# A row sum on one core: the first 128 rows as two loads of half rows

## The chip, the cores and the metric

The kernel runs on one core of a Trainium2 chip. The metric is the device time of one execution in microseconds, the median of several runs. Beside it there is one profiled execution with a trace of every instruction and every DMA packet.

## The reference

The input `x` has 32 x 512 rows of 1024 float32 numbers, 64 MiB in all. Each row is summed and the sum is multiplied by 0.5; the output has 32 x 512 numbers.

```python
def reference(x: np.ndarray, multiplier: float) -> np.ndarray:
    return (np.sum(x, axis=-1) * multiplier).astype(np.float32)
```

## The kernel before, in words

The 16384 rows are taken as 128 partitions x 128 rows. They are worked on in three parts.

**The head** is the first 128 rows, one row for each partition (L112). One load brings it into the tile `head`. ScalarE sums each partition's row with an activation that scales and accumulates (`act_row`, L90) into the first column of the tile `column`, which VectorE has cleared (L113). So that 128 sums can leave in long runs rather than one number for each partition, VectorE transposes `column` in blocks of 32 x 32 into `row` (L117). Of `row`, partitions 0, 32, 64 and 96 then hold 32 sums each, and one store of 4 x 32 numbers brings them out (L188).

**The blocks.** Seven blocks follow: the first of 15 rows for each partition, the others of 16 (64 KiB for each partition). They go through three buffers `xb`. VectorE sums a whole block in one reduction (L136) and scales the sums into `res` (L142); of the seventh block VectorE takes the first eight rows and ScalarE the other eight. The load of a block waits until VectorE has freed the buffer three blocks earlier (`freed`).

**The end.** The eighth block comes in five pieces, smaller and smaller: three into the buffer (`landed_p0` to `landed_p2`) and two into the tile `end` (`landed_e0`, `landed_e1`). Its rows are shared between ScalarE (`act_row`) and VectorE (`dve_sum`, L99, a fused add and reduction). The very last row is cut into three parts that VectorE sums one after the other; the last instruction of the chain is `final`.

All loads and stores are issued by SP, in program order on one queue, with no planner in between. `start_loads_at_entry` (L223) moves those leading loads that wait for nothing (the head and the first three blocks) to the start of the program. After the last load SP issues the early store of the blocks' sums (L184, which waits for VectorE and ScalarE), the head's store (L188), and then the last store (L214), for which it waits until the last sums are there. It ends by waiting for all three stores.

Of the kernel before, what the change touches and what calls it, by code (L numbers as in the profile page):

```python
# [9 lines left out]
def kernel(  # L10
# [13 lines left out]
    nc = tc.nc  # L24
# [4 lines left out]
    P = nc.NUM_PARTITIONS  # L29
    fp32 = mybir.dt.float32  # L30
    ADD = mybir.AluOpType.add

    x_flat = x.flatten_outer_dims()
    N, D = x_flat.shape
    rows = N // P
    out_flat = out.rearrange("b s -> (b s)")
# [5 lines left out]
    Q = 32  # L42
# [1 line left out]
    own = 1 + sum(sizes)  # L44
    x_rows = x_flat[P : P * own, :].rearrange("(p c) d -> p c d", p=P)
    x_last = x_flat[P * own : N, :].rearrange("(p c) d -> p c d", p=P)
    out_head = out_flat[0:P].rearrange("(q c) -> q c", c=Q)
    out_rows = out_flat[P : P * own].rearrange("(p c) -> p c", p=P)
    out_last = out_flat[P * own : N].rearrange("(p c) -> p c", p=P)

    def sbuf(name, *shape):
        return ctx.enter_context(nc.sbuf_tensor(name, list(shape), fp32)).ap()
# [2 lines left out]
    buf = [sbuf(f"xb{i}", P, B, D) for i in range(bufs)]  # L55
    sums = sbuf("sums", P, rows)
    res = sbuf("res", P, rows)
    head = sbuf("head", P, 1, D)
    column = sbuf("column", P, Q)
    row = sbuf("row", P, Q)  # L60
    cuts = [384, 736, D]
    at = 368
    end = sbuf("end", P, at + D - cuts[1])

    def sem(name):
        return nc.alloc_semaphore(name=name)

    dve_done = sem("dve_done")
# [3 lines left out]
    def marks(i, engine):  # L72

        s = dve_done if engine == "dve" else act_done
        i.then_inc(s, 1)
        counts[engine] += 1
        return counts[engine]

    def load(name, dst, src, free=None, behind=None):

        landed = sem(name)
        i = nc.sync.dma_start(out=dst, in_=src)  # L82
        if free is not None:
            i.wait_op(dve_done, free, "sem-ge")
        if behind is not None:
            i.wait_op(behind, 16, "sem-ge")
        i.then_inc(landed, 16)
        return landed

    def act_row(t, r, dst):  # L90
        return nc.scalar.activation(  # L91
            out=t[:, r, :],
            in_=t[:, r, :],
            func=mybir.ActivationFunctionType.Copy,
            scale=mul,
            accum_out=dst,
        )
# [11 lines left out]
            accum_out=dst,  # L109
        )  # L110

    landed_head = load("landed_head", head[:, 0, :], x_flat[0:P, :])  # L112
    cleared = marks(nc.vector.memset(column, 0.0), "dve")  # L113
    nc.scalar.wait_ge(landed_head, 16)
    nc.scalar.wait_ge(dve_done, cleared)
    summed = marks(act_row(head, 0, column[:, 0:1]), "act")
    turned = nc.vector.transpose(out=row, in_=column)  # L117
    turned.wait_op(act_done, summed, "sem-ge")
    marks(turned, "dve")

    freed = []
    blocks = []
    for b, n in enumerate(sizes):
# [9 lines left out]
        h = n if b < n_blocks - 2 else n // 2  # L133
# [3 lines left out]
                out=sums[:, c0 : c0 + h], in_=t[:, 0:h, :], axis=mybir.AxisListType.X  # L137
# [5 lines left out]
            out=res[:, c0 : c0 + h],  # L143
            in_=sums[:, c0 : c0 + h],
            scalar=mul,
            op=mybir.AluOpType.mult,
# [33 lines left out]
            )  # L180
        )
    ]
    nc.sync.wait_ge(dve_done, early_dve)
    early = nc.sync.dma_start(out=out_rows, in_=res[:, 1:own])  # L184
    early.wait_op(act_done, early_act, "sem-ge")
    early_stored = sem("early_stored")
    early.then_inc(early_stored, 16)
    first = nc.sync.dma_start(out=out_head, in_=row[0:P:Q, :])  # L188
    first_stored = sem("first_stored")
    first.then_inc(first_stored, 16)  # L190

    summed_up = sem("summed_up")
    on_act = {1, 4, 7, 9, 13, 14}
# [22 lines left out]
    stored = sem("stored")  # L216
    store.then_inc(stored, 16)
    nc.sync.wait_ge(early_stored, 16)
    nc.sync.wait_ge(first_stored, 16)
    nc.sync.drain()  # L220
    nc.sync.wait_ge(stored, 16)

# [62 lines left out]
```

## Time and profile before

| What | Value |
|---|---|
| median of 3 runs | 160.5 us (160.48 to 160.57) |
| profiled execution, its own time | 160.47 us |
| its span in the trace | 159.2 us |
| moved by DMA | 67.18 MB, mean 422 GB/s over the span |
| time to landing of the head's load | 3.3 us from issue |
| time to landing of the first block's load | 21.2 us from issue |

The span is the part of the execution that the trace covers, from the first instruction to the last; the remaining 1.27 us lie around it. In the profile, DVE is VectorE, ACT is ScalarE, and SPq is the queue of SyncE that issues DMAs. Landing is counted from the issue of a DMA to the moment at which its semaphore is complete. A DMA of 128 partitions is spread over 16 DMA engines, and here each partition's contiguous run is one packet in the trace; every load adds one completion packet of 4 bytes on each of its engines. A share of busy time over 100% in a short stretch comes from counting packets with the stretch in which they start.

### The profile page before, as it was taken

The page shows a single profiled execution, that of the slowest core. Times are in us where ns is not written, and L with a number is a line of the kernel's source. Part 1 is how long each engine was busy: PE and PEld are TensorE (multiplying, and loading weights), DVE is VectorE, ACT ScalarE, POOL GpSimd, SP SyncE. Part 2 cuts the span into 40 slices and gives each one's busy share as a digit, 9 for nine tenths or more (in the row PEclk, how much of TensorE's full clock was granted, in tenths as well). Part 3 has the DMA queues.
Part 4 walks back from the last instruction along what each step waited for, and adds up shares of the span by engine and source line. Part 5 has one row for each costly group of instructions (what it writes and reads, how often), then busy time and mean ns, then how long its engine had stood idle before and what let it go on. Part 6 is the DMA issues. An engine that isn't in the chain of part 4 may idle for free.

```text
span 159.2 us, 131 instructions
## 1 busy us (share of the span) xinstructions
DVE 119.1 (75%) x40; ACT 17.4 (11%) x31; POOL 0.2 (0%) x4
## 2 busy tenths in 40 slices
DVE  0000059995799968999599995999959999598376
ACT  2300000000000000000000000000000000397384
POOL 0000000000000000000000000000000000000000
DMA  9997996996997999969969969969989799798994
GB/s 379 494 401 340 494 527 264 527 527 264 527 461 329 527 395 395 527 280 511 527 264 527 527 264 527 494 296 527 445 346 527 346 445 527 329 453 371 420 401 151
DMA packets 2168, 67.18 MB, mean 422 GB/s; under 512 B 504, under 2 KB 760, under 8 KB 1016
## 3 DMA queue, kind: packets, MB, share of 16 engines
q1 hardware_dynamic: 2168, 67.18, 98.0%
HBM read 67.11 MB, written 0.07 MB: 422 GB/s over the span
## 4 chain that ended last, share of the span: by engine, by line
DMA 74%; DVE 24%; another core or an unknown queue 1%; SPq 1%; issue 0%
DMA xb<-in_x_dram 74%; DVE sums L136 22%; DVE xb L101 1%; SPq L82 1%; DVE end L101 0%; DVE res L142 0%; DVE res L101 0%
## 5 line engine op out<-in xcount | busy, mean ns | idle before, releaser
L136 DVE TENSOR_REDUCE sums<-xb 128x16 f32<-128x16384 f32 (+2 forms) x7 | 110.9, 15849 | 28.4 <-DMA xb<-in_x_dram 28.4
L91 ACT ACTIVATE xb<-xb 128x1024 f32<-128x1024 f32 x14 | 14.6, 1045 | 137.1 <-DMA xb<-in_x_dram 137.1
L101 DVE CUSTOM_DVE_ANT_0 xb<-xb 128x512 f32<-128x512 f32 (+1 forms) x10 | 5.9, 652 | 4.4 <-DMA xb<-in_x_dram 4.4
L91 ACT ACTIVATION_READ_ACCUMULATOR xb<-xb 128x1 f32 x14 | 2.6, 187 | 0.0
L113 DVE MEMSET column<- 128x32 f32 x1 | 0.1, 85 | 3.0 <-PEq L26 3.0
L117 DVE STREAM_TRANSPOSE row<-column 128x32 f32<-128x32 f32 x1 | 0.2, 212 | 2.6 <-ACT head L91 2.6
L91 ACT ACT_TABLE_LOAD x1 | 1.3, 1283 | 3.1 <-DVE column L113 3.1
L142 DVE TENSOR_SCALAR res<-sums 128x16 f32<-128x16 f32 (+2 forms) x7 | 1.2, 174 | 0.2
L91 ACT ACTIVATE head<-head 128x1024 f32<-128x1024 f32 x1 | 1.1, 1056 | 0.0
L101 DVE DVE_READ_ACCUMULATOR2_ANT res<- 128x1 f32 x10 | 0.8, 80 | 0.0
L101 DVE CUSTOM_DVE_ANT_0 end<-end 128x176 f32<-128x176 f32 (+1 forms) x2 | 0.7, 326 | 0.0
L91 ACT ACTIVATION_READ_ACCUMULATOR head<-head 128x1 f32 x1 | 0.2, 186 | 0.0
L101 DVE DVE_READ_ACCUMULATOR2_ANT end<- 128x1 f32 x2 | 0.2, 82 | 0.0
L266 POOL MEMSET const-bfloat16-1.0<- 128x1 bf16 x1 | 0.1, 101 | 0.0
L266 POOL MEMSET const-uint8-127<- 128x1 uint8 x1 | 0.1, 101 | 0.0
L266 POOL MEMSET const-float32-0.0<- 128x1 f32 x1 | 0.1, 98 | 0.2 <-issue 0.2
L266 POOL MEMSET const-float32-1.0<- 128x1 f32 x1 | 0.1, 98 | 0.0
## 6 DMA issues: line engine op xcount, KB each, us to landing
xb<-in_x_dram SPq DMA_DIRECT2D x1, 7680.0 KB, 21.2
xb<-in_x_dram SPq DMA_DIRECT2D x1, 5120.0 KB, 33.6
xb<-in_x_dram SPq DMA_DIRECT2D x1, 2048.0 KB, 36.4
xb<-in_x_dram SPq DMA_DIRECT2D x1, 704.0 KB, 20.8
head<-in_x_dram SPq DMA_DIRECT2D x1, 512.0 KB, 3.3
end<-in_x_dram SPq DMA_DIRECT2D x1, 176.0 KB, 19.2
end<-in_x_dram SPq DMA_DIRECT2D x1, 144.0 KB, 10.8
xb<-in_x_dram SPq DMA_DIRECT2D x6, 40.8
```

The lines of the kernel that those rows point to most:

```text
L82: i = nc.sync.dma_start(out=dst, in_=src)
L91: return nc.scalar.activation(out=t[:, r, :], in_=t[:, r, :], func=mybir.ActivationFunctionType.Copy, scale=mul, accum_out=dst,)
L101: return nc.vector.tensor_tensor_reduce(out=row[:, 0:mid], in0=row[:, 0:mid], in1=row[:, mid:], scale=scale, scalar=0.0, op0=ADD, op1=ADD, ...
L113: cleared = marks(nc.vector.memset(column, 0.0), "dve")
L117: turned = nc.vector.transpose(out=row, in_=column)
L136: nc.vector.reduce_sum(out=sums[:, c0 : c0 + h], in_=t[:, 0:h, :], axis=mybir.AxisListType.X),
L142: scaled = nc.vector.tensor_single_scalar(out=res[:, c0 : c0 + h], in_=sums[:, c0 : c0 + h], scalar=mul, op=mybir.AluOpType.mult,)
L266: nc = _bacc.Bacc("TRN2", target_bir_lowering=False, num_devices=1)
```

## The change

The head comes in by two loads of 64 rows. In each, a partition receives half a row (512 numbers, 2 KB), so that partition `p` of load `h` holds half `p % 2` of row `64 h + p // 2`. ScalarE sums the halves with two activations, one for each load, into the first two columns of `column`. VectorE transposes as before; the sums of the two halves of a row now stand beside each other in one partition of `row`, and one more VectorE addition joins neighbours into `joined`. Two stores of 4 x 16 numbers bring the sums out. They are issued ahead of the early store and its wait, where the one store came behind it. ScalarE waits for VectorE's clearing before it waits for the loads. Both head loads wait for nothing, so they stand at the start of the program, ahead of the three block loads.

```diff
-    out_head = out_flat[0:P].rearrange("(q c) -> q c", c=Q)
+    H = 2
+    half = D // H
+    out_head = out_flat[0:P].rearrange("(h q c) -> h q c", h=H, c=Q // H)
...
-    head = sbuf("head", P, 1, D)
+    head = sbuf("head", P, H, half)
     column = sbuf("column", P, Q)
     row = sbuf("row", P, Q)
+    joined = sbuf("joined", P, Q // H)
...
-    landed_head = load("landed_head", head[:, 0, :], x_flat[0:P, :])
+    landed_head = [
+        load(
+            f"landed_h{h}",
+            head[:, h, :],
+            x_flat[h * P // H : (h + 1) * P // H, :].rearrange("r (s d) -> (r s) d", s=H),
+        )
+        for h in range(H)
+    ]
     cleared = marks(nc.vector.memset(column, 0.0), "dve")
-    nc.scalar.wait_ge(landed_head, 16)
     nc.scalar.wait_ge(dve_done, cleared)
-    summed = marks(act_row(head, 0, column[:, 0:1]), "act")
+    for h in range(H):
+        nc.scalar.wait_ge(landed_head[h], 16)
+        summed = act_row(head, h, column[:, h : h + 1])
+    summed = marks(summed, "act")
     turned = nc.vector.transpose(out=row, in_=column)
     turned.wait_op(act_done, summed, "sem-ge")
-    marks(turned, "dve")
+    turned = marks(turned, "dve")
+    pairs = row.rearrange("p (c s) -> p c s", s=H)
+    both = nc.vector.tensor_tensor(
+        out=joined.rearrange("p (c o) -> p c o", o=1),
+        in0=pairs[:, :, 0:1],
+        in1=pairs[:, :, 1:2],
+        op=ADD,
+    )
+    both.wait_op(dve_done, turned, "sem-ge")
+    marks(both, "dve")
...
+    first_stored = sem("first_stored")
+    for h in range(H):
+        first = nc.sync.dma_start(out=out_head[h], in_=joined[h:P:Q, :])
+        first.then_inc(first_stored, 16)
     nc.sync.wait_ge(dve_done, early_dve)
     early = nc.sync.dma_start(out=out_rows, in_=res[:, 1:own])
     early.wait_op(act_done, early_act, "sem-ge")
     early_stored = sem("early_stored")
     early.then_inc(early_stored, 16)
-    first = nc.sync.dma_start(out=out_head, in_=row[0:P:Q, :])
-    first_stored = sem("first_stored")
-    first.then_inc(first_stored, 16)
...
-    nc.sync.wait_ge(first_stored, 16)
+    nc.sync.wait_ge(first_stored, 16 * H)
```

## The prediction

> **What bounds the kernel now.** I read first the page's busy and queue lines.
>
> ```profile
> span 159.2 us, 131 instructions
> DVE 119.1 (75%) x40; ACT 17.4 (11%) x31; POOL 0.2 (0%) x4
> ...
> q1 hardware_dynamic: 2168, 67.18, 98.0%
> ```
>
> The 16 DMA engines work 98.0% of the span: 156.0 of 159.2 us. No other engine is near that. The missing 3.2 us must be at the two ends, since the answer for DMA from 0 to 1.1 us counts no packet at all, and the time after 157.1 us holds little but the last store. So the time is: start of the stream, plus its length, plus a tail. The start, from the timeline (start, length, engine, line, operation):
>
> ```profile
> 0.00 0.39 SPq L82 DMA_DIRECT2D head<-in_x_dram  x1
> 0.44 1.38 SPq L82 DMA_DIRECT2D xb<-in_x_dram  x3
> 3.12 1.28 ACT L91 ACT_TABLE_LOAD   x1 [3.12 <-DVE column L113]
> 4.41 1.06 ACT L91 ACTIVATE head<-head 128x1024 f32<-128x1024 f32 x1
> 5.59 0.21 DVE L117 STREAM_TRANSPOSE row<-column 128x32 f32<-128x32 f32 x1 [2.56 <-ACT head L91]
> ```
>
> SP issues a load every 0.46 us (1.38 / 3); the first packet starts 1.11 us after the first issue. All compute on `head` is over by 5.8 us. Then the waits:
>
> ```profile
> ACT xb L91 <- DMA xb<-in_x_dram: 137.1, 4, 132.2
> DVE sums L136 <- DMA xb<-in_x_dram: 28.4, 7, 15.8
> ```
>
> VectorE next waits up to 15.8 us for the first block, and ScalarE 132.2 us for its first block row. Last, the end in the timeline:
>
> ```profile
> 147.33 0.64 SPq L188 DMA_DIRECT2D out_dram<-row  x1
> 154.77 0.69 DVE L101 CUSTOM_DVE_ANT_0 xb<-xb 128x512 f32<-128x512 f32 x1 [1.13 <-DMA xb<-in_x_dram]
> 157.36 0.31 DVE L101 CUSTOM_DVE_ANT_0 end<-end 128x145 f32<-128x145 f32 x1
> 157.70 0.34 SPq L214 DMA_DIRECT2D out_dram<-res  x1
> ```
>
> VectorE goes without a pause from the landing of the second last-block piece (154.77) to 157.67, and the very last load lands at 157.27 (issued 146.47, 10.8 us to landing), 0.09 us before the instruction that needs it. Both ends of the tail hang on the stream: a delay of the whole stream passes to the end one for one.
>
> **Prices of the stream.** Two stretches of the DMA view give the cost of a small packet, one the cost of a start. From 22 to 38 us (64 KB packets only), 155.9 to 156.5 us (pieces of 1 to 1.5 KB), and 1.1 to 2.0 us (4 KB packets of `head`), in that order:
>
> ```profile
> DMA packets 106, 6.95 MB, mean 434 GB/s; under 512 B 0, under 2 KB 0, under 8 KB 0
> ```
> ```profile
> DMA packets 204, 0.22 MB, mean 371 GB/s; under 512 B 32, under 2 KB 204, under 8 KB 204
> ## 3 DMA queue, kind: packets, MB, share of 16 engines
> q1 hardware_dynamic: 204, 0.22, 103.5%
> ```
> ```profile
> DMA packets 67, 0.27 MB, mean 305 GB/s; under 512 B 0, under 2 KB 0, under 8 KB 67
> ```
>
> Full rate is 434 GB/s, 27.1 bytes per ns and engine. In the second stretch 16 x 0.6 us x 1.035 = 9.94 us of engine time moved 371 x 0.6 = 222.6 KB, worth 8.21 us at full rate; 1.73 us is left over 204 packets: **8.5 ns a packet** besides its bytes. In the third, 0.9 us at 305 in place of 434 GB/s lost 0.9 x (1 - 305/434) = **0.27 us**: the price of the start.
>
> **The change, part by part.**
>
> *More packets.* The 128 packets of 4 KB become 256 of 2 KB, the bytes stay: 128 x 8.5 / 16 = 0.068 us for each engine, and one more completion packet for each engine, another 0.009. Together +0.08 us. [...]
>
> *A second small load in the start.* Does the stream run dry between the two? The second is issued at 0.44 us, so by the first's 1.11 us its packets can start at 1.55. The first holds 8 packets for each engine, 8 x (2048 / 27.1 + 8.5) = 0.67 us, so it lasts to 1.78 us, or 2.05 with the start's loss: cover of 0.23 to 0.50 us. The block loads move back by one issue, 0.46 us; the first can start at about 0.90 + 1.11 = 2.01, and the halves last to 2.45 us or more: cover of 0.44. If either cover is gone, the stream stands still for the shortfall. But the start's loss itself may grow. No row shows a load of small rows following another at the start. Lower bound: the first packets are half as long, so a part of the loss that goes with packet length may halve, -0.13 us. Upper bound: the second load repeats the loss, +0.27. I take half of it, +0.13, since the loss belongs to the first half microsecond (in the windows view 254 GB/s from 1.1 to 1.6 us, 369 from 1.6 to 2.1), where packets will now be twice as many.
>
> *ScalarE and VectorE.* ScalarE does two activations of 512 in place of one of 1024 (1.06 us and 0.19 for reading the sum): between 1.4 and 2.5 us in all. VectorE gets one addition of 128x16, by the nearest row (L142, 128x16, 0.17 us) about 0.2, behind a wait for its own transpose. Behind these waits on VectorE stands the first block's sum, whose data comes at about 21 us; behind the second activation stands ScalarE's row at 139.85. All of it, with the later start of ScalarE by one issue, is over near 8 us: 13 us of cover, so nothing. Without cover it would be about 1 us.
>
> *The stores of the first rows.* They go before the early store and ahead of its wait, two in place of one: 2 x 0.64 us of SP from 146.80, and the early store is issued near 148.1 instead of 146.91. What comes behind them on SP is the last store, for which SP now waits 9.7 us. All loads are issued before them, and the early store's packets wait behind those until 156.4, so 8 us of cover; without it, up to 1.2 us. Four more packets of 64 bytes and four completions lie behind the last load in the queues and done before the last store at 158.5. Nothing.
>
> *Sum:* 0.08 + 0.13 = +0.21 us on the profiled execution's 160.47 us (span 159.2 and 1.27 around it, which the change has no reason to move): 160.68. The median of the runs is 160.50, 0.03 over the profiled one: **160.7 us**. About 0.2% (0.32 us) is what a measurement of this kernel can tell from no change, so this counts as the same.
>
> **The rivals.**
>
> *The start is paced by packets, not by bytes (slower).* If in the first half microsecond or so an engine gets packets at a fixed pace, as when a 4 KB packet's turn of about 0.16 us (4096 / 27.1 + 8.5) is also the turn of a 2 KB one, each such turn loses 0.08 us. For: the 254 GB/s of the first half microsecond. Against: in the tail 1 to 1.5 KB packets pass at their own 8.5 ns plus bytes, and the last store's 128 packets of 64 bytes all pass between 158.5 and 158.8 us; but the tail's were queued 10 us ahead. It decides from about 3 lost turns (0.24 + 0.08 = 0.32). Six of the first eight give 0.48 + 0.08 = +0.56: 161.1 us; all 16, +1.3: 161.8. A whole second start loss, 0.27 + 0.08 = +0.35, gives 160.9 and belongs here too. Chance 0.38.
>
> *Every load pays its fixed part (slower).* `head` takes 3.3 us to land, 1.2 of it bytes at full rate: 2.1 us fixed. Bare on the stream, a second load would cost +2.1 + 0.08: 162.7. Against it: 13 loads at that price would leave the engines idle for 27 us, and they idle 3.2. Chance 0.02. [...]
>
> *The start gets smoother (faster).* Shorter packets could take away all the start's loss and even out the engines: -0.27 + 0.08 = -0.19, and the last engine goes over from `head` to the first block at 2.93 us where the mean is 2.73 (packet records of the trace); if the small packets close that, -0.2 more: 160.1 us. For: the end waits for the slowest engine. Against: it needs both, and more packets to the same bytes. Chance 0.14.
>
> **The numbers.** The forecast, +0.21 with bounds -0.05 (0.08 - 0.13) to +0.32, has 0.46, and its own range is 160.4 to 160.8 us. Rivals: 0.40 slower, 0.14 faster. The range goes down to 160.3 (half of the faster case's way) and up to 161.3, beyond the six-turn case, and leaves out the far ends of the three rivals, about 2 in 10.
>
> **What would show it.** Right: 128 packets more of 2 KB, the DMA share still 98% with a first half microsecond no slower than 254 GB/s, the first block landing about 0.2 us later, the last store issued near 157.9 us, and VectorE unbroken before it. A gap between the two halves, or a first block that lands over 0.35 us later, shows the slower rival; one that lands earlier, the faster one. I am wrong altogether if the first block lands as forecast and the end has moved otherwise: then the tail or the moved stores hold a cost that I put at nothing.

## The result, and the profile after

The changed kernel takes 162.82 us (median of 6 runs, 162.06 to 163.84), the kernel before 160.53 us beside it (160.48 to 160.57): 1.0152 times as long, 95% interval 1.0128 to 1.0175, or +2.29 us. It has also become unsteady: its runs lie 1.8 us apart, those of the kernel before 0.1. The profiled execution is one of the longer ones, 163.57 us, 3.10 above the profiled 160.47 of before; the profile's differences are to be held against that. In the ratios of this document a run more than 1.5% above the fastest of its kernel counts as slow and is left out; that is one run each of e4 and e9.

The page's busy and queue lines after:

```profile
span 162.2 us, 136 instructions
DVE 119.3 (74%) x41; ACT 17.6 (11%) x33; POOL 0.2 (0%) x4
...
q1 hardware_dynamic: 2320, 67.18, 96.6%
```

The compute engines work as long as before (VectorE 119.3 us and ScalarE 17.6, before it was 119.1 and 17.4). The DMA engines are busy for 96.6% of a longer span: 156.7 us in place of 156.0, but the idle part has grown from 3.2 to 5.5 us. The timeline says where in the program that can be:

```profile
0.00 0.86 SPq L85 DMA_DIRECT2D head<-in_x_dram  x2
0.91 1.38 SPq L85 DMA_DIRECT2D xb<-in_x_dram  x3
3.41 1.28 ACT L94 ACT_TABLE_LOAD   x1 [3.41 <-PEq L26]
4.70 0.63 ACT L94 ACTIVATE head<-head 128x512 f32<-128x512 f32 x1
6.31 0.18 DVE L133 TENSOR_TENSOR joined<-row 128x16 f32<-128x16 f32 x1
...
149.92 1.19 SPq L206 DMA_DIRECT2D out_dram<-joined  x2
157.87 0.69 DVE L104 CUSTOM_DVE_ANT_0 xb<-xb 128x512 f32<-128x512 f32 x1 [1.14 <-DMA xb<-in_x_dram]
160.45 0.31 DVE L104 CUSTOM_DVE_ANT_0 end<-end 128x145 f32<-128x145 f32 x1
160.80 0.34 SPq L236 DMA_DIRECT2D out_dram<-res  x1
```

The head's compute is over by 6.5 us, as forecast. From the start of the last VectorE chain (157.87) to the start of its last piece (160.45) it is 2.58 us, before it was 2.59 (154.77 to 157.36): the tail is the same, 3.1 us later. So all of the loss lies ahead of it. The waits and the time to landing of the first block (7680 KB) put it right at the start:

```profile
DVE sums L157 <- DMA xb<-in_x_dram: 30.8, 7, 18.2
```
```profile
xb<-in_x_dram SPq DMA_DIRECT2D x1, 7680.0 KB, 23.8
```

The same line of the kernel before:

```profile
xb<-in_x_dram SPq DMA_DIRECT2D x1, 7680.0 KB, 21.2
```

The first block lands 23.8 us after its issue at 0.91, at 24.7; before, it was 21.2 after 0.44, at 21.6. These 3.1 us are the whole difference. It is not a matter of all 16 engines. The trace's packet records show when each engine starts the block. The records do not name the engine; a packet of 61440 bytes that starts where another one ends (as at 2.89 + 2.31 = 5.20 us) is taken for the same engine's second, and the sixteen that follow no other such packet are the engines' first ones. Before, these start between 2.59 and 2.93 us; after, fifteen start between 2.64 and 3.30 and **the sixteenth at 6.16 us**. The count of packets in flight says the same: about ten from 2.8 to 3.1 us, fifteen from 3.3 to 6.1, sixteen from then on, where before it was about sixteen all this time. So one engine stands still for about 3 us. The first packets also take longer, 2.71 us in the mean and up to 3.34, where before it was 2.34 and at most 2.46. The block's last packets end between 20.83 and 21.27 us before, and between 21.41 and 24.38 after: the last engine is 3.11 us late, the mean one 1.00. No engine takes over another's rows (each moves eight of the block's 128 packets), so the lag stays: the program's last load ends at 156.88 before and 159.93 after, 3.04 us apart.

### The profile page after: what moved, and what is told of

It is laid out like the page before. It is cut to its first block, busy times and chain, and to the rows that moved or that the text cites. A ratio compares the mean times of both kernels' runs of the same rounds, so it can differ in the third digit from the quotient of the medians.

```text
span 162.2 us, 136 instructions
## 1 busy us (share of the span) xinstructions
DVE 119.3 (74%) x41; ACT 17.6 (11%) x33; POOL 0.2 (0%) x4
## 2 busy tenths in 40 slices
DMA packets 2320, 67.18 MB, mean 414 GB/s; under 512 B 528, under 2 KB 784, under 8 KB 1168
## 3 DMA queue, kind: packets, MB, share of 16 engines
q1 hardware_dynamic: 2320, 67.18, 96.6%
## 4 chain that ended last, share of the span: by engine, by line
DMA 74%; DVE 23%; another core or an unknown queue 1%; SPq 1%; issue 0%
DMA xb<-in_x_dram 74%; DVE sums L157 21%; DVE xb L104 1%; SPq L85 1%; DVE end L104 0%; DVE res L163 0%; DVE res L104 0%
## 5 line engine op out<-in xcount | busy, mean ns | idle before, releaser
L94 ACT ACTIVATE head<-head 128x512 f32<-128x512 f32 x2 | 1.2, 620 | 0.0
## 6 DMA issues: line engine op xcount, KB each, us to landing
xb<-in_x_dram SPq DMA_DIRECT2D x1, 7680.0 KB, 23.8
```

The costliest lines, as they stand in the source:

```text
L94: return nc.scalar.activation(out=t[:, r, :], in_=t[:, r, :], func=mybir.ActivationFunctionType.Copy, scale=mul, accum_out=dst,)
```

## The experiments

Each run's time is held against the kernel before beside it, 160.50 to 160.58 us in the median. The first theory, D: the first block's load is issued 0.46 us later, the head no longer holds enough work, and engines run dry. Against it stood P (the 2 KB packets) and Q (five loads in a row).

**e1. One load, 2 KB packets (kernel before).**

```diff
-    head = sbuf("head", P, 1, D)
+    head = sbuf("head", P, 2, D // 2 + 16)[:, :, 0 : D // 2]
...
-    landed_head = load("landed_head", head[:, 0, :], x_flat[0:P, :])
+    landed_head = load("landed_head", head, x_flat[0:P, :].rearrange("p (s d) -> p s d", s=2))
```

> The kernel before, but the head's one load writes two half rows with a gap between them in each partition, so that its packets are 2 KB (256 of them) while the number of loads and stores stays. Theory D (the engines run out of work between the small loads and the first block, because the first block's load is issued one issue, 0.46 us, later): here the first block's load is issued at 0.44 us as in the kernel before, so no engine pauses; 160.5 to 160.8 us, 0.07 of it for packets. Rival P (2 KB packets in the start disturb the stream by themselves): one engine starts the first block some 2 us after the others and the time is about 162.8 us, with runs up to 1 us apart.

161.03 us (160.96 to 161.15), ratio 1.0028 (1.0018 to 1.0038). Issuing it takes 0.69 us and the first packet starts at 1.60 us in place of 1.11; that 0.49 us is about the 0.45 us lost. The engines start the block at 3.12 to 3.56 us, 0.53 to 0.63 later than in the kernel before, so none pauses for long. P falls.

**e2. Two small loads with 4 KB packets (kernel before; the first block's first row for each partition by its own load).**

```diff
+            landed_lead = load("landed_lead", t[:, 0:1, :], x_rows[:, 0:1, :])
```

> The kernel before, with the first row of the first block for each partition taken out into a load of its own ahead of the rest: five loads before the program's entry ends, as in the changed kernel, but both small loads have 4 KB packets, and together they hold 2.4 us of work in place of 1.2. Theory D: the large load is issued 0.46 us later but covered by 1.2 us more work, so no engine pauses: 160.5 to 160.7 us. Rival Q (five loads issued in a row are too many for the queues, or each further load pays a start): about 162.8 us, with a pause in the stream before the first large packets.

160.99 us (160.65 to 161.73), ratio 1.0039 (1.0013 to 1.0065). The large load is issued third and at 0.91 us, just as in the changed kernel, but behind 1 MB in place of 0.5. Its first packets start together (4.01 to 4.50 us; the second small load lands at 4.7) and take 2.12 us each but for one. Neither a further load in the start nor the third place at 0.91 us costs 2 us by itself: together they cost 0.41. The runs are unsteady by 1 us, and the trace has packets of up to 0.82 us among the small ones.

**e3. The changed kernel with the third block's load held back.**

```diff
-            freed[b - bufs] if b >= bufs else None,
+            freed[b - bufs] if b >= bufs else (cleared if b == 2 else None),
```

> The changed kernel, with the third block's load held back until VectorE has cleared its column (about 3.4 us), 40 us before its data is needed: four loads at the entry in place of five. Theory D: the first block's load is issued at 0.91 us as in the changed kernel, so the pause stays: about 162.8 us. Rival Q (five loads in a row): the pause goes, 160.6 to 160.8 us.

163.1 us (161.97 to 163.55), ratio 1.0145 (1.0107 to 1.0184). Q falls.

**e4. A load of 64 bytes between head and first block (kernel before).**

```diff
+    spare = sbuf("spare", 1, 16)
+    tiny = load("landed_tiny", spare, x_flat[0:1, 0:16])
```

> The kernel before, with a load of 64 bytes into one spare partition issued between the head's load and the first block's: SP issues the first block's load some 0.4 to 0.6 us later, the engines get next to no more work, and all packets of the head stay 4 KB. Theory D: several engines pause between the head and the first block and the time comes to 161.5 to 163 us, unsteady from run to run. Rival P (2 KB packets): no change, 160.5 to 160.6 us. Rival Q (five loads) expects about 162.8 us too; e2 and e3 tell it from D.

161.34 us in the median of ten, from 160.47 to 162.92; ratio without the longest 1.0036 (1.0015 to 1.0057). Nothing but a load of 64 bytes, 0.32 us of issue, was put ahead of the block; one run loses 2.3 us, three lose nothing, the others lie between. In the profiled one, at 161.33 us, no engine paused for more than about 0.2 us, yet the block's first packets took up to 3.37 us. So D's run-dry queue is not needed for a loss of 0.8 us.

The next question was how long the block's load takes to get ready (L), and whether compute or stores matter (W).

**e5. The two head loads joined, all else as changed.**

```diff
-    landed_head = [
-        load(
-            f"landed_h{h}",
...
+    landed_both = load(
+        "landed_both",
+        head,
+        x_flat[0:P, :].rearrange("(h r) (s d) -> (r s) h d", h=H, s=H),
+    )
+    landed_head = [landed_both] * H
```

> The changed kernel with its two head loads joined into one DMA that places the same half rows in the same partitions: ScalarE, VectorE and the stores are those of the changed kernel, only the number of head loads is that of the kernel before. Theory L (the first block's data needs some 1.8 us from the end of its issue, and what the head loads hold no longer covers that): the issue of one load of 256 packets takes about 0.7 us and so delays the start, but no engine waits for the first block; 160.9 to 161.2 us, as for the one load of 2 KB packets in the kernel before. Rival W (the moved stores, the added addition or the halved activations cost the time): about 162.8 us.

160.79 us (160.72 to 160.87), ratio 1.0013 (1.0003 to 1.0022). The halves, the addition, the moved stores and the 2 KB packets together cost 0.22 us; **the other 2.1 us come with the second load.** W falls. SP's issues and the block's landing in this kernel, from the timeline and the DMA view:

```profile
0.00 0.45 SPq L85 DMA_DIRECT2D head<-in_x_dram  x1
0.50 1.40 SPq L85 DMA_DIRECT2D xb<-in_x_dram  x3
```
```profile
xb<-in_x_dram SPq DMA_DIRECT2D x1, 7680.0 KB, 21.3
```

The block's issue is back at 0.50 us, and its time to landing at 21.3, before it was 21.2.

**e6. The first block's load between the two head loads.**

> The changed kernel with the first block's load issued between the two head loads, at 0.44 us as in the kernel before. Theory D as first put (only the 0.46 us later issue matters): the time comes back to 160.6 to 160.9 us. Theory L (what counts is the time from the first block's issue to the moment when the work ahead of it is drained): only half as much work lies ahead, drained near 1.9 us, 1.0 us after the issue in place of 1.2 to 1.8: still exposed, 162.3 to 164 us.

```diff
+        if h == 0:
+            landed_first = load(
+                "landed0", buf[0][:, 0 : sizes[0], :], x_rows[:, 0 : sizes[0], :]
+            )
```

160.96 us (160.81 to 161.32), ratio 1.0026 (1.0017 to 1.0035). The same five loads in another order, and all but 0.39 of the 2.29 us are back. Here are the timeline's issues and the block's landing:

```profile
0.44 0.42 SPq L85 DMA_DIRECT2D xb<-in_x_dram  x1
0.91 0.43 SPq L85 DMA_DIRECT2D head<-in_x_dram  x1
```
```profile
xb<-in_x_dram SPq DMA_DIRECT2D x1, 7680.0 KB, 21.0
```

Its packets start on the engines at 2.02 to 2.38 us, 1.6 to 1.9 us after the issue. In the changed kernel the same load is issued 0.47 us later, and from 2.8 to 3.1 us, 1.9 to 2.2 us after its issue, some six engines still stand idle for it. L, as I put it, is wrong: a fixed lead time doesn't explain both.

**e7 and e8. A touch of 64 bytes for each partition ahead of all loads**, in e7 from the block's rows, in e8 from the head's.

```diff
+    touched = load("touched", spare, x_rows[:, 0, 0:16])
```

> The changed kernel with one more load ahead of all others: 64 bytes for each partition from the beginning of the first block's own rows, into a spare tile. It moves every load back by one issue (0.46 us). Theory T (the delay of the first block is a first touch of its rows: the 128 runs lie 444 KB apart over 58 MB, the head's lie in 512 KB): the touch takes that delay, behind which the head's packets wait a little; the first block's packets then start at once and the time is 160.9 to 161.4 us, steadier. Rival L alone (the delay belongs to any first large load, touched or not): the lead is the same as in the changed kernel, so 163.0 to 163.5 us.

> As the run before, but the 64 bytes for each partition come from the beginnings of the head's own rows, so that nothing of the first block is touched ahead: issue, packets and bytes are the same. Theory T: no cure, 163.0 to 163.5 us. Rival L alone: the same as the touch of the block, within 0.3 us.

162.47 us (162.03 to 162.93) and 162.64 us (162.45 to 162.96); ratios 1.0116 (1.0094 to 1.0138) and 1.0129 (1.0113 to 1.0144). Both lose, and the two can't be told apart. The touch is no cure; L alone had asked for 163.0 us or more, and both stay below that.

**e9. The joined load of e5, and a 64-byte load between it and the block.**

```diff
+    tiny = load("landed_tiny", spare, x_flat[0:1, 0:16])
```

> The kernel with the two head loads joined into one (160.79 us), with the load of 64 bytes into one partition between it and the first block's load: the first block is issued third and near 0.85 us, as in the changed kernel (0.91), but only 257 rows in two loads lie ahead, one of them a single row. Theory G (the queue makes a load ready in series after its issue, about 0.75 us for each load of 128 rows, slower than the 0.46 us at which SP issues; a single row costs next to nothing): the first block is ready in time or nearly so, 160.8 to 161.6 us. Rival D (what counts is that the first block is issued at 0.9 us rather than 0.45): about 162.8 us.

162.47 us in the median of ten, from 160.84 to 163.38; ratio without the longest 1.0102 (1.0068 to 1.0137). SP's issues:

```profile
0.50 0.35 SPq L85 DMA_DIRECT2D spare<-in_x_dram  x1
0.90 1.29 SPq L85 DMA_DIRECT2D xb<-in_x_dram  x3
```

Against e5 a load of 64 bytes stands ahead of the block, whose issue has moved from 0.50 to 0.90 us and from second to third place, and most of the loss is there again, though three of the ten runs lose under 0.7 us. That is D's time and not G's. The traced execution, the longest, has thirteen engines that start the block by 3.04 us and three that start it at 3.77, 4.47 and 5.78. The load of 64 bytes adds two packets in all (2306 against 2304), so its own packets can hardly hold up three engines.

**e10. Two head loads of 64 partitions, 4 KB rows (kernel before).**

```diff
-    landed_head = load("landed_head", head[:, 0, :], x_flat[0:P, :])
+    landed_head = [
+        load(f"landed_h{k}", head[k:P:2, 0, :], x_flat[k:P:2, :]) for k in range(2)
+    ]
```

> The kernel before, with the head's rows split over two loads of 64 partitions each (even and odd partitions), rows of 4 KB as before: three loads up to the first block, which is issued third at 0.91 us as in the changed kernel, but the two hold 64 rows each, 128 in all. Theory G: two loads of 64 rows take no longer to make ready than one of 128, so the first block is in time: 160.6 to 161.1 us. Rivals D and S (the third load in a queue has to wait for the first to be done): about 162.8 us, with pauses ahead of the first block's packets.

162.85 us (162.54 to 163.7), ratio 1.0155 (1.0125 to 1.0185). No half rows at all, the same total of rows, and the loss is that of the change. G falls. (SP's two issues took 1.19 us here, so the block was issued at 1.24 and not at 0.91.) The split of one load into two of 64 partitions costs 2.35 us here.

**e11. The first block's load held until VectorE has cleared its column (kernel before).**

```diff
+            freed[b - bufs] if b >= bufs else (cleared if b == 0 else None),
```

> The kernel before, with the first block's load held back until VectorE has cleared its column (issued near 3.1 us): the engines run dry between the head (done near 2.9 us) and the first block (first packets near 4.2 us). If a pause costs only its own length, the gap of some 1.3 us makes it 161.8 to 162.0 us, steady from run to run. If an engine that has run dry pays a restart on top (theory R, by which a pause of 0.2 to 0.4 us became 2.3 us in the changed kernel), it is 163 to 165 us, unsteady, with one or a few engines starting the block 1 to 2 us after the rest.

161.6 us (161.47 to 162.09), ratio 1.0074 (1.0058 to 1.009). The issue came at 1.64 us, earlier than I had thought. The engines started the block between 2.71 and 3.90 us, and some had run dry, since the head had landed by 3.23. The traced execution loses 1.6 us: its last engine starts 1.0 us later than in the kernel before, and the first packets take 0.6 us longer in the mean (2.94 us). So R, which asked for 163 us or more and single engines 1 to 2 us behind the rest, falls in that form, but the pause isn't all that is paid. That an issue at 1.64 us behind one load costs 1.1 us, less than one at 0.91 behind two, also speaks against D.

**e12. The changed kernel with the first block's load from ScalarE's queue.**

```diff
+    nc.scalar.dma_start(out=buf[0][:, 0 : sizes[0], :], in_=x_rows[:, 0 : sizes[0], :]).then_inc(
+        landed_first, 16
+    )
```

> The changed kernel with the first block's load issued by ScalarE's queue at the program's start, beside the two head loads on SP's: nothing is ahead of it in its own queue, and its packets take turns with the head's. Theories G, D and S all expect the pause gone: 160.5 to 161.0 us. If it stays at 162.5 us or more, the delay belongs to the first block's data (its rows in memory), not to the queue, and all three fall.

160.69 us (160.64 to 160.92), ratio 1.0013 (1.0004 to 1.0023). The block is issued at 0.12 us and all but 0.19 us of the loss is gone, with both small loads in place. From its timeline:

```profile
0.00 0.86 SPq L85 DMA_DIRECT2D head<-in_x_dram  x2
0.12 0.36 ACTq L116 DMA_DIRECT2D xb<-in_x_dram  x1
```

Then theory H: a load issued while data already flows is late. The first packet starts at 1.0 to 1.6 us in these kernels.

**e13 and e14. A head load twice as long; in e14 the block's load is held back as in e11.**

```diff
-    head = sbuf("head", P, 1, D)
+    head = sbuf("head", P, 2, D)
...
+            freed[b - bufs] if b >= bufs else (cleared if b == 0 else None),
```

> The kernel before, with a head load twice as long: one load also brings the next 128 rows into a second half of the tile, which nobody uses (0.5 MB more, 128 packets of 4 KB: 1.2 us of stream, plus 0.1). The first block is issued near 0.45 us, behind 2.5 us of work. All theories: 161.8 to 162.0 us, steady. It is the control for the next run.

> The control with the first block's load held back as in the run with the block held (issued near 1.65 us, while the head's packets flow and 2 us before the engines are through with them); it is the second load in its queue. Theory H (a load issued while data already flows at full rate needs up to 4 us from issue to the first packet on its slowest engine; one issued before the flow begins does not): some engines pause and start the block 1 to 2 us late, 162.8 to 164.5 us, unsteady. Rival K (a load of rows is ready at most 2.3 us after its issue, as in the run with the block held, and only the third load in a queue is late): ready by 3.9 us, before the head is drained, so within 0.2 us of the control.

161.94 us (161.88 to 162.0) and 162.66 us (162.56 to 163.06); ratios 1.0088 (1.0073 to 1.0103) and 1.0138 (1.0122 to 1.0153). With the block issued at 1.69 us in e14, in place of 0.50 in e13, the kernel takes 0.72 us longer, although the head holds enough work until 4.2 us or later. But no engine starts the block late (4.22 to 4.82 us, with the head landed at 5.0; in e13 4.33 to 4.46 and 4.8): the cost is in packets that take longer (4 KB ones up to 1.19 us and 209 ns in the mean, 185 in e13; the block's first ones 2.52 us in the mean, in e13 all sixteen 2.27). K is wrong, and H only half right: a late issue costs even under cover, but not by the pauses that it foretold, and less.

**e15. The kernel before, with the block from ScalarE's queue.** The edit is that of e12.

> The kernel before, with the first block's load issued by ScalarE's queue at the program's start, beside the head's load on SP's. It is the version that could beat both: if the start of the kernel before still holds some of the same pause (its cover was not wide), 160.2 to 160.4 us; if it holds none, 160.4 to 160.6.

160.64 us (160.49 to 160.79), ratio 1.0004 (0.9995 to 1.0014): no difference that can be told. No version here beats the kernel before.

**e16. The changed kernel, first block from rows that lie together.**

```diff
+    x_near = x_flat[P : P * (1 + sizes[0]), :].rearrange("(p c) d -> p c d", p=P)
```

> The changed kernel, with the first block's load reading 15 x 128 rows that lie together (7.5 MB) in place of runs of 60 KB that lie 444 KB apart over 58 MB; the first block's sums are therefore those of other rows, all else is as it was. Theory T in a second form (the block's far-apart rows make its first packets late, and 64 bytes of each were not enough to touch them): 160.6 to 161.2 us. Theory H: no cure, 162.2 to 163.5 us.

163.19 us (161.96 to 163.57), ratio 1.0155 (1.0104 to 1.0205). T falls for good.

**e17. The changed kernel, second and third block held back.**

```diff
+            freed[b - bufs] if b >= bufs else (after_head if b == 1 else None),
```

> The changed kernel, with the second and third blocks' loads held back until VectorE has joined the head's sums (about 6.5 us; the second block's data is due at 21 us): the first block's load, third at 0.91 us, is the last that is issued while the start's packets flow. Theory H (the first block's own load, issued when data already flows, is late): 162.3 to 163.3 us, with late and slow first packets as before. Rival M (the loads issued behind it, at 1.4 to 2.3 us, make the first block's packets late or slow): 160.6 to 161.2 us.

163.3 us (162.92 to 163.62), ratio 1.0164 (1.0142 to 1.0186), and the traced execution again has engines that start the block late, at 3.63 and 4.48 us. M falls: the first block's own load is the one that is late.

**e18. The changed kernel, first block held until the head has landed.**

```diff
             freed[b - bufs] if b >= bufs else None,
+            landed_head[1] if b == 0 else None,
```

> The changed kernel, with the first block's load held back until the second head load has landed (near 3.35 us), so that it is issued 2.4 us later than in the changed kernel but into idle engines. Theory H (the lateness belongs to a load that is issued while others' data flows): its first packets start about 1.1 us after its issue on all engines, within 0.4 us of each other; the engines stand idle for some 1.6 us, and the time is 162.0 to 162.5 us, steadier than the changed kernel's and not longer, for all the later issue. Rival D (the later the issue, the worse): 164 us or more.

163.08 us (162.81 to 163.15), ratio 1.0155 (1.014 to 1.017), with these issues:

```profile
0.00 0.86 SPq L85 DMA_DIRECT2D head<-in_x_dram  x2
...
3.11 1.28 SPq L85 DMA_DIRECT2D xb<-in_x_dram  x3
```

Issued 2.2 us later than in the changed kernel, the block makes the program end only 0.3 us later. The engines start within 0.8 us of each other, at 4.09 to 4.86; no straggler. That is against D and for H. But the first packets are slow here too (2.96 us in the mean), with the head's packets all done by 2.80 us, and the time is 0.6 to 1.1 us above H's. H does not hold as I put it.

What the packet records show across all runs (times in us; place is the block's place in its queue; start and length are those of each engine's first packet of the first block in the traced execution; the last column is the median of the runs):

| kernel | place | block issued | starts on the engines | mean length | median |
|---|---|---|---|---|---|
| e12, from ScalarE's queue | 1 | 0.12 | 1.93 to 2.34 | 2.46 | 160.69 |
| e15, before, from ScalarE's queue | 1 | 0.12 | 2.34 to 2.54 | 2.40 | 160.64 |
| before | 2 | 0.44 | 2.59 to 2.93 | 2.34 | 160.53 |
| e6, block between | 2 | 0.44 | 2.02 to 2.38 | 2.54 | 160.96 |
| e5, head joined | 2 | 0.50 | 2.66 to 3.18 | 2.42 | 160.79 |
| e13, long head | 2 | 0.50 | 4.33 to 4.46 | 2.27 | 161.94 |
| e1, 2 KB packets | 2 | 0.73 | 3.12 to 3.56 | 2.33 | 161.03 |
| e4, 64 bytes between | 3 | 0.81 | 2.68 to 3.12 | 2.61 | 161.34 |
| e9, joined and 64 bytes | 3 | 0.90 | 2.74 to 5.78 | 2.51 | 162.47 |
| after | 3 | 0.91 | 2.64 to 6.16 | 2.71 | 162.82 |
| e3, third block later | 3 | 0.91 | 2.76 to 4.82 | 3.28 | 163.1 |
| e16, rows together | 3 | 0.91 | 2.96 to 4.52 | 3.02 | 163.19 |
| e17, other blocks later | 3 | 0.91 | 2.71 to 4.48 | 2.77 | 163.3 |
| e2, 1 MB ahead (56 KB packets) | 3 | 0.91 | 4.01 to 4.50 | 2.13 | 160.99 |
| e10, two loads of 64 | 3 | 1.24 | 2.83 to 5.24 | 2.97 | 162.85 |
| e7, touch of the block | 4 | 1.38 | 3.36 to 3.97 | 2.74 | 162.47 |
| e8, touch of the head | 4 | 1.38 | 3.33 to 4.09 | 2.51 | 162.64 |
| e11, block held | 2 | 1.64 | 2.71 to 3.90 | 2.94 | 161.6 |
| e14, long head, held | 2 | 1.69 | 4.22 to 4.82 | 2.52 | 162.66 |
| e18, after the head | 3 | 3.11 | 4.09 to 4.86 | 2.96 | 163.08 |

The seven kernels that issue the block by 0.73 us have it steady: the engines start within 0.6 us of each other, with first packets of 2.27 to 2.54 us. The six that issue it third, at 0.90 to 1.24 us, behind the head's 512 KB alone, have engines that start it 1.5 us or more after the first ones. e4, third at 0.81, is steady in its traced execution, though not in its times. e2 issues it third at 0.91, but behind 1 MB, and starts it within 0.5 us. Of those that issue it later still, none has starts more than 1.2 us apart, but all lose time, e14 against its control e13.

**What is shown and what is open.** Shown: the loss is the late and slow start of the first block's packets, carried to the end by the slowest engine, and it comes and goes with the moment, the order and the queue in which that one load is issued (e5, e6, e9, e12) and with what lies ahead of it (e2). It is not the half rows (e10), the packets' size (e1), the compute, the stores (e5), the place of the rows in memory (e16) or the loads behind (e3, e17). Open: what in the chip makes a load issued at 0.9 us so much slower to start than one issued at 0.44. The runs do not separate the moment from the place either: single engines straggle only where the block is third in its queue (e11 and e14 have it second, later, and show none), though the third place is not enough (e2, e18). In the kernel before, the very first packet comes 0.72 us after its issue ended (1.11 less 0.39); the block's first ones in the changed kernel come 1.3 to 4.8 us after theirs (issue ended at 1.34).

## Why the prediction was wrong

**The step that failed** is the second one, a second small load in the start. It took the time from issue to first packet, 1.11 us, from the one load that is issued into an idle chip, and used it for the third load. Measured on the third, it is 1.7 us on the first engine, up to 2.4 on the next fourteen, some of which stood idle by then, and 5.2 on the last (2.64, 3.30 and 6.16 less 0.91). The halves lasted to 3.15 us at most, so the "cover of 0.44" was not there on that last engine, and by my own words the stream then stands still for the shortfall: about 3 us. The prediction gave the condition but priced it at nothing. Why the third load needs so long stays open, as said above.

**The term was also taken as a mean over the engines.** The upper bound of 0.27 us is a rate lost by all sixteen. What the end sees is the slowest: 3.11 us in the profiled execution where the mean lag was 1.00. The faster rival had "the end waits for the slowest engine" in it; the slower one, and the bounds, left it out.

**The rivals.** "The start is paced by packets" asked for a slower first half microsecond, and it was slower, in the windows view 254 GB/s before (first line) and 143 after (the other two):

```profile
1.10:1.60 0.50, 0.00 (x0) 0.00 (x0) 0.00 (x0) 1.00 0.90 254
```
```profile
1.10:1.60 0.50, 0.00 (x0) 0.00 (x0) 0.00 (x0) 1.00 1.01 143
1.60:2.10 0.50, 0.00 (x0) 0.00 (x0) 0.00 (x0) 1.00 0.95 365
```

But e5 moves the same 256 packets in 160.79 us and has its head drained at 2.87 us, where the kernel before took to 2.93, so it isn't this that costs 2 us. The prediction's own sign for this rival, a first block that lands over 0.35 us later, was there too (3.1 us) and did not mean it. "Every load pays its fixed part" named 162.7 us, close to the 162.82 by number only: e12 has the same loads and pays 0.19, and e6 0.39. The direction, slower, had 0.40, the forecast "same" 0.46, and the range ended at 161.3, since no case in it had an engine standing still for 3 us.

**What held.** The tail passes the delay on one for one (2.59 and 2.58 us). The moved stores cost nothing: SP's two took 1.19 us from 149.92, 9 us ahead of need. The added addition took 0.18 us (forecast 0.2) and the second activation was over by 6.0 us. Packets and compute together are within e5's 0.22 us; I had 0.08 for the packets. The count of packets rose from 2168 to 2320: 128 of 2 KB and 24 small ones of the added load and stores.

## What to carry to other kernels

Where a stream fills the whole time, look at the order and the moment of the first few issues: issue the large load early, and let nothing that goes ahead of it push back its issue, however little it moves (64 bytes cost 1.7 us in e9 against e5), unless it holds the engines busy for long enough (the 1 MB of e2 did, and the kernel lost 0.41 us). The time from issue to first packet of a load into an idle chip (1.11 us) was no measure for one issued behind others (1.7 to 5.2 us on the 16 engines of the changed kernel). And price a pause in the start by the slowest DMA engine (3.11 us late here, the mean one 1.00), since each had a fixed share of the block, eight packets of 128, and nothing evened them out up to the end (3.04 us late).

## What the runs showed of the hardware that was not expected

- One load of 64 bytes, put ahead of the first block so that its issue came 0.4 us later (e9 against e5), cost 1.7 us in the median and made the time spread over 2.5 us.
- A single engine of 16 can start a load 2.9 us after the next slowest (6.16 and 3.30 us in the changed kernel), and the last load of the program still ends 3.04 us late.
- Issuing the block's load from another engine's queue (e12) removed all but 0.19 us of the loss with both small loads left as they were.
- The issue itself differs: 0.69 us for 128 x 2 x 512 into rows with a gap (e1), 0.45 for the joined load (e5), 0.6 for a load of 64 partitions with every other one left out (e10), 0.39 for the plain one. The issues of the three block loads, unchanged, took 1.54 us behind that of e1, 1.53 behind those of e10 and 1.38 behind the plain one, so it is not the shape of a load alone.
